# A transformer block pair on one core: low parts on GpSimd in the attention, filling products' splits later, a new opening, spread value products, sums between k-tiles

## The chip, the core and the metric

The kernel runs on one core of a Trainium2 chip. It has TensorE (PE in the profile, with PEld for its weight loads), VectorE (DVE), ScalarE (ACT), GpSimd (POOL) and the DMA queues, here those of SyncE (SP), ScalarE and GpSimd. The metric is the time of one execution on the device in microseconds.

## What is computed

Two transformer blocks on 512 tokens of width 1024. The first has a sparse attention, then a cross attention over 256 memory tokens, then a gated feed-forward network. With 512 tokens every selected block and every window covers all earlier tokens, so two of the attention's three branches are plain causal attentions over two sets of keys and values.

```python
h = rmsnorm(x, norm_mix_w)
q, kc, vc, ks, vs, kw, vw, gl = split(h @ nsa_w_in)          # 16 heads of 64, 4 groups of keys
gates = sigmoid(gl)                                          # three per head and token
k_cmp, v_cmp = gelu(blocks(kc) @ ck_w1) @ ck_w2, gelu(blocks(vc) @ cv_w1) @ cv_w2
o = gates[0] * softmax(q k_cmp) v_cmp + gates[1] * softmax(q ks) vs + gates[2] * softmax(q kw) vw
x = x + o @ nsa_w_out
x = x + memory_cross_attention(rmsnorm(x), rmsnorm(mem))     # ca_wq, ca_wkv, ca_wo
x = x + (silu(causal_conv3(h @ gate)) * (h @ val)) @ ffn_w_down
x = rmsnorm(x)
# second block
u, v, za, ab, ab_gate, zb, g_a, g_b = split(rmsnorm(x) @ w_in_2 + b_in)
merged = sigmoid(g_a) * (spatial_gating(u, v, za) @ w_pa) + sigmoid(g_b) * (conv31_branch(ab, ab_gate, zb) @ w_pb)
x = x + merged @ w_out
x = x + sigmoid(rmsnorm(x) @ w_ple_gate) * (p @ w_ple)
out = rmsnorm(x)
```

## The kernel before

Activations are kept transposed, 128 features on the partitions and 512 tokens in the free dimension, so a width of 1024 is a list of eight tiles, the k-tiles of a product. Every float32 operand `x` of a large product is split in two rounded parts: the high part by ScalarE, the low part (`x` less the high part) by VectorE. `mm` adds three products: high by high, high by low, low by high. `dense` (L196) makes one tile of 512 columns from eight k-tiles, 24 products.

`weight` (L163) loads a piece of 128 x 1024 into one of three raw buffers (`wr`), and ScalarE makes the high part (`wh`). The low part (`wl`) goes to GpSimd or VectorE by a running count of pieces: `eng = nc.gpsimd if self.pieces % 4 < self.share else nc.vector`. `share` is 0 at first, 4 in the second block from its start to the `w_pa` products, and 0 after them.

The RMS norms are put behind the products: the tile of squares is summed over features by one-column products with a tile of ones (`token_sum`, L219), GpSimd takes the power -0.5 (`rsqrt`), and TensorE transposes the result to all partitions (`bcast`), which ScalarE copies to SBUF as `rb`. `stat` does the sum and the power.

The opening (`nsa`, L287) loads x and the first two weight pieces in halves of 512 columns, on SyncE's and ScalarE's queues; for each of eight k-tiles it splits x and runs two products into `pk`, with the squares of x made two k-tiles later. Then come weight piece 10, the last squares, the product `px[0]`, `stat` into `rt`, the product with piece 11, and `rb`. `shifted` (L329) scales and shifts `pk` and `px`; `cmp_keys` (L394) and `cmp_values` (L409) compress them with four weight pieces each, and call one function of a list after each piece: keys, queries, `token_gates` and `gates_turned` (L358) in the one, `values` (L436) in the other, which accumulates over its four calls in four PSUM banks.

The attention has 32 units, two per head. `stage_a` (scores, minimum, exponential, and a multiplication by gate over denominator on GpSimd), `stage_b` (TensorE transposes, then splits) and `stage_c` (products with the values) are staggered: at step s of the loop, `stage_a` has been called up to unit s + 2, `stage_b` is called for s and `stage_c` for s - 1. Other work is called at set steps (`FILL`, L42) ahead of `stage_b`: the remaining queries and keys, `mem_init`, `mem_keys` (L715) and `mem_values` (L731). A filling job runs its product and directly behind it takes it out of PSUM and splits it.

The order of instructions on each engine is not that of the program alone. A planner at build time takes, for an engine that its costs say is free, the ready instruction that stands first in the program. The order is then fixed, and each engine runs its list in order. The program's place is a priority. All instructions are recorded by one helper, so the profile shows one line (L95) for nearly everything, and tile names tell the groups apart.

`residual` (L748) adds a product to x, splits the result and adds up its squares on GpSimd; its followers (`cross` L767, `ffn_up` L857, `block2` L882) run a first `dense` and then `stat`, in `block2` by `norms` (L888) for two sets of squares.

Of the kernel before, what the change touches and what calls it, by code (L numbers as in the profile page):

```python
# [17 lines left out]
P = 128  # L18
# [102 lines left out]
class Body:  # L121
# [74 lines left out]
    def dense(self, src, rhs, n=S, raw=None):  # L196
# [22 lines left out]
    def token_sum(self, acc, n):  # L219
# [7 lines left out]
        return ps  # L227

# [24 lines left out]
    def setup(self):  # L253
# [9 lines left out]
        nc.vector.memset(self.ones, 1.0)  # L263
        self.neghalf = c.tile([P, 8], F32, name="neghalf")
# [22 lines left out]
    def nsa(self):  # L287
# [17 lines left out]
        acc = []  # L305

        def square(k):
            sq = self.a()
            nc.scalar.activation(sq, x[k], AF.Square)
            if k < 2:  # L310
                acc.append(sq)
            else:
                (nc.vector if k % 2 else nc.gpsimd).tensor_tensor(acc[k % 2], acc[k % 2], sq, op=ALU.add)

        pk = [self.ps(), self.ps()]
        for k in range(KD):
            xs.append(self.split(x[k], self.vec("norm_mix", k)))
            if k % 4 == 0:
                w = [self.split(t[:, k * P:k * P + S]) for t in w0]
            s = slice(k % 4 * P, k % 4 * P + P)  # L320
            for j in range(2):
                self.mm(pk[j], (w[j][0][:, s], w[j][1][:, s]), xs[k], k == 0, k == KD - 1)
            if k >= 2:
                square(k - 2)
# [139 lines left out]

        def keys(b, pair):
            p = self.dense([I["nsa_w_in"][12 + 2 * b + pair]], xs)
            f = self.a()
            nc.vector.tensor_tensor(f, p, rb, op=ALU.mult)
            for u in range(2):
                s = slice(u * 64, u * 64 + 64)  # L470
                h, l = self.a(dt=F32R), self.a(dt=F32R)
                so = slice(64 - u * 64, 128 - u * 64)
                nc.scalar.copy(h[s], f[s])
                nc.vector.tensor_sub(l[s], f[s], h[s].bitcast(F32))
                for t in (h, l):
                    nc.gpsimd.dma_start(t[so].bitcast(F32), t[s].bitcast(F32))
                del t
                K[b, 2 * pair + u] = (h, l)
# [3 lines left out]
        def queries(m):  # L482
            p = self.dense([I["nsa_w_in"][m]], xs)
            f = F[m] = self.a()
            nc.vector.scalar_tensor_tensor(f, p, -0.125, rb, op0=ALU.mult, op1=ALU.mult)
            for u in range(2):
                q = self.a(dt=F32R)
                s = slice(u * 64, u * 64 + 64)
                so = slice(64 - u * 64, 128 - u * 64)
                nc.scalar.copy(q[s], f[s])  # L490
                nc.vector.tensor_sub(q[so], f[s], q[s].bitcast(F32))
                Q[2 * m + u] = q
# [124 lines left out]
        w = self.weight(I["nsa_w_in"][10], raw)  # L617
        del raw
        square(KD - 2)
        square(KD - 1)  # L620
        nc.vector.tensor_tensor(acc[0], acc[0], acc.pop(), op=ALU.add)
        px = [self.ps()]
        for k in range(KD):
            s = slice(k * P, (k + 1) * P)
# [687 lines left out]
```

## Time and profile before

| what | us |
|---|---|
| median of 3 runs | 1444.14 (1443.67 to 1444.43) |
| the profiled execution | 1447.17 |
| its span, first to last instruction | 1445.4 |
| TensorE busy | 1413.7 (98%) |
| VectorE busy | 924.0 (64%) |
| ScalarE busy | 644.9 (45%) |
| GpSimd busy | 421.1 (29%) |
| mean granted TensorE clock | 0.994 |

The span is shorter than the execution's time, which also has what lies around the first and last instruction. A product counts as busy until its modelled end, about 390 ns for 512 columns, though the next may start 227 ns after it; so a busy TensorE isn't one at its peak, and the number of products in a stretch tells more.

### The profile page before, as it was taken

The numbers are of one execution on the slowest core, as the hardware profiler recorded it, in microseconds if no ns is written. First come the engines' busy times: TensorE is split into PE (matmuls) and PEld (weight loads), VectorE is DVE, ScalarE is ACT, GpSimd is POOL, SyncE is SP. The second block draws the span as 40 slices with busy tenths as digits, with TensorE's granted clock in tenths as the row PEclk, the third lists the DMA queues.
The fourth block names the chain that finished last, engine by engine and source line by source line (L and its number), as shares of the span: only waits on it lengthen the run. The fifth ranks groups of instructions, "written<-read, shape, count | busy, mean of one in ns | idle before, by whom it ended". The sixth has DMA issues, their size and how long they took to land.

```text
span 1445.4 us, 18570 instructions
## 1 busy us (share of the span) xinstructions
PE 1413.7 (98%) x7010; PEld 1189.7 (82%) x7010; DVE 924.0 (64%) x1551; ACT 644.9 (45%) x1113; POOL 421.1 (29%) x367
## 2 busy tenths in 40 slices
PE   8899989999999999999999999999999999999997
PEld 6787878988888888888888888888887888888897
DVE  5958999996455455655543227995978574444564
ACT  5467768784344332332333234223244554432452
POOL 2222556551210221111111124544455440011223
PEclk9999999999999999999999999999999999999999
DMA  6531121214312323233233332332322222332331
GB/s 209 160 117 59 34 70 59 74 36 158 99 59 88 102 88 102 89 102 99 90 95 98 94 123 87 117 102 74 101 76 86 88 88 88 104 100 92 98 102 59
DMA packets 42681, 136.14 MB, mean 94 GB/s; under 512 B 5600, under 2 KB 8032, under 8 KB 42592
## 3 DMA queue, kind: packets, MB, share of 16 engines
q1 hardware_dynamic: 39856, 129.98, 28.8%
q0 software_dynamic: 1152, 3.15, 0.8%
q10 hardware_dynamic: 1584, 1.84, 0.4%
q8 instruction: 55, 0.90, 0.2%
q14 instruction: 34, 0.28, 0.1%
HBM read 129.70 MB, written 2.10 MB: 91 GB/s over the span
## 4 chain that ended last, share of the span: by engine, by line
PE 90%; DVE 6%; ACT 1%; issue 1%; POOL 1%; DMA 0%; SPq 0%; POOLq 0%; ACTq 0%; DVEq 0%
PE ps L95 90%; DVE a L95 4%; DVE wl L95 1%; ACT a L95 1%; POOL a L95 0%; DMA wr<-in_nsa_w_in_dram 0%; DVE ps L95 0%; ACT wh L95 0%; DVE s L95 0%; POOL wl L95 0%; SPq L95 0%; POOLq L1307 0%; POOL s L95 0%; DVE wh L95 0%; ACTq L95 0%
## 5 line engine op out<-in xcount | busy, mean ns | idle before, releaser
L95 PE MATMUL ps<-a,wh 128*128 128x512 f32 (+1 forms) x3120 | 954.8, 387 | 0.0
L95 PEld LDWEIGHTS ps<-a,wh 128*128 128x128 f32 x3120 | 581.4, 188 | 114.3 <-issue 0.5
L95 PE MATMUL ps<-a,wl 128*128 128x512 f32 (+1 forms) x1552 | 599.8, 386 | 1.4 <-POOL wl L95 1.4
L95 ACT CAST wh<-wr 128x1024 fp32r<-128x1024 f32 (+1 forms) x224 | 233.4, 1044 | 510.0 <-PE ps L95 314.9
L95 DVE TENSOR_TENSOR a<-ps,a 128x512 f32<-128x512 f32 (+6 forms) x292 | 173.8, 610 | 264.2 <-PE ps L95 209.8
L95 PEld LDWEIGHTS ps<-a,wl 128*128 128x128 f32 x1552 | 292.0, 188 | 59.5 <-POOL wl L95 1.8
L95 POOL TENSOR_TENSOR a<-a,a 128x512 f32<-128x512 f32 (+1 forms) x102 | 130.6, 1284 | 576.6 <-ACT a L95 461.4
L95 DVE TENSOR_TENSOR wl<-wr,wh 128x1024 fp32r<-128x1024 f32 x168 | 216.9, 1293 | 123.2 <-ACT wh L95 122.0
L95 PE MATMUL ps<-a,a 128*128 128x256 f32 (+4 forms) x1204 | 212.9, 323 | 7.9 <-ACT a L95 7.4
L95 PEld LDWEIGHTS ps<-a,a 128*128 128x128 f32 x1204 | 171.0, 192 | 26.0 <-ACT a L95 13.5
L95 POOL TENSOR_TENSOR wl<-wr,wh 128x1024 fp32r<-128x1024 f32 x56 | 134.8, 2409 | 167.1 <-ACT wh L95 167.1
L95 DVE SCALAR_TENSOR_TENSOR ps<-a,vecs,ps 128x501 f32<-128x501 f32 (+25 forms) x240 | 167.6, 736 | 3.2
L95 POOL TENSOR_TENSOR a<-a,s 128x512 f32<-128x512 f32 (+3 forms) x140 | 115.6, 853 | 174.2 <-DVE s L95 87.1
L95 DVE TENSOR_TENSOR a<-a,a 128x512 fp32r<-128x512 f32 (+3 forms) x168 | 116.4, 699 | 35.9 <-ACT a L95 25.0
L95 ACT CAST a<-a 128x512 fp32r<-128x512 f32 (+1 forms) x116 | 71.6, 621 | 82.6 <-DVE a L95 68.3
L95 ACT ACTIVATE a<-a 128x512 f32<-128x512 f32 (+1 forms) x114 | 61.9, 550 | 92.9 <-DVE a L95 92.6
L95 PE MATMUL ps<-wh,a 128*128 128x512 f32 (+1 forms) x320 | 94.9, 376 | 1.2 <-ACT a L95 1.2
L95 ACT ACTIVATE a<-ps,s 128x256 f32<-128x256 f32 (+4 forms) x148 | 77.5, 528 | 28.1 <-DVE s L95 25.3
L95 DVE SCALAR_TENSOR_TENSOR a<-a,vecs,a 128x511 f32<-128x511 f32 (+3 forms) x92 | 75.5, 824 | 4.3 <-ACT a L95 3.5
L95 ACT CAST a<-ps 128x384 fp32r<-128x384 f32 (+2 forms) x132 | 62.9, 488 | 33.3 <-PE ps L95 28.3
L95 PEld LDWEIGHTS ps<-wh,a 128*128 128x128 f32 x320 | 59.8, 194 | 12.0 <-ACT a L95 1.6
L95 PE MATMUL ps<-ident,a 128*128 128x128 f32 x372 | 56.8, 276 | 9.3 <-DVE a L95 8.6
(81 smaller groups left out, 677.2 us busy)
## 6 DMA issues: line engine op xcount, KB each, us to landing
wr<-in_w_in_dram SPq DMA_DIRECT2D x56, 512.0 KB, 3.6
wr<-in_ffn_gate_dram SPq DMA_DIRECT2D x22, 512.0 KB, 3.6
wr<-in_ffn_val_dram SPq DMA_DIRECT2D x22, 512.0 KB, 3.6
wr<-in_ffn_d_dram SPq DMA_DIRECT2D x16, 512.0 KB, 3.5
wr<-in_nsa_w_in_dram SPq DMA_DIRECT2D x14, 512.0 KB, 3.7
wr<-in_ca_wk_dram SPq DMA_DIRECT2D x8, 512.0 KB, 3.5
wr<-in_ca_wv_dram SPq DMA_DIRECT2D x8, 512.0 KB, 3.6
wr<-in_nsa_w_out_dram SPq DMA_DIRECT2D x8, 512.0 KB, 3.5
```

What stands on the lines that cost most here:

```text
L95: return lambda *a, **k: f(*[_raw(x) for x in a], **{n: _raw(x) for n, x in k.items()})
```

## The change

Constants: `FILL` loses its first entry and some steps move up; `SHARE` gets two more values, 1 for `cmp_keys` and `cmp_values` and 4 for the attention loop; after the loop the share is 0 again. Setup runs nine products of `ones` into a PSUM tile that nothing reads. In the opening the first two weight pieces come in columns 0 to 256, 256 to 512 and 512 to 1024, and the squares move behind weight piece 10. The transposes for `rb` stand behind the fifth k-tile of the second product.

```diff
-FILL = (0, 2, 8, 10, 4, 6, 12, 14, 14, 15, 17, 20, 23, 26, 30)
+FILL = (1, 8, 10, 3, 5, 12, 14, 14, 15, 17, 20, 23, 26, 30)
-SHARE = (4, 0)
+SHARE = (4, 0, 1, 4)
...
+        idle = self.ps((P, P))
+        for _ in range(9):
+            nc.tensor.matmul(idle, self.ones, self.ones, start=True, stop=True)
...
-        for c, ks in ((slice(0, S), (2, 4)), (slice(S, 2 * S), (5, 6, 7))):
+        chunks = {0: (0, 256), 2: (256, 512), 4: (512, 1024)}
+        for k, ks in ((0, (2,)), (2, (4,)), (4, (5, 6, 7))):
+            c = slice(*chunks[k])
             for i in range(2):
                 nc.sync.dma_start(w0[i][:, c], I["nsa_w_in"][8 + i][:, c])
-            for k in ks:
-                nc.sync.dma_start(x[k], I["x"][k])
+            for j in ks:
+                nc.sync.dma_start(x[j], I["x"][j])
...
+        px, acc = [], []
+        for j in range(2):
+            w = self.weight(I["nsa_w_in"][10 + j], raw)
+            raw = None
+            if j == 0:
+                for k in range(KD):
+                    sq = self.a()
+                    nc.scalar.activation(sq, x[k], AF.Square)
+                    if k < 2:
+                        acc.append(sq)
+                    else:
+                        (nc.vector if k % 2 else nc.gpsimd).tensor_tensor(acc[k % 2], acc[k % 2], sq, op=ALU.add)
...
+            px.append(self.ps())
+            for k in range(KD):
+                s = slice(k * P, (k + 1) * P)
+                self.mm(px[j], (w[0][:, s], w[1][:, s]), xs[k], k == 0, k == KD - 1)
+                if j == 1 and k == 4:
+                    rb = self.to_sbuf(self.bcast(rt, NT))
+            if j == 0:
+                self.stat(acc, out=rt)
```

`keys`, `queries`, `mem_keys` and `mem_values` run their products and return a function `rest`, which takes the result out of PSUM and splits it. In the loop `rest` is called behind `stage_b` and `stage_c`. `values(0)` moves into `cmp_keys`, the others one call forward, `gates_turned` into `cmp_values`, and `queries(2)` out of the loop. In `mem_keys` the sum of squares moves ahead of the products.

```diff
+            rests = [f(*args) for f, args in fill.get(s, [])]
             stage_b(s)
             if s:
                 stage_c(s - 1)
+            for rest in rests:
+                if rest:
+                    rest()
...
-        cmp_keys(ck, [lambda: keys(1, 0), lambda: queries(1), token_gates, gates_turned])
+        self.share = SHARE[2]
+        cmp_keys(ck, [lambda: keys(1, 0)(), token_gates, lambda: queries(1)(), lambda: values(0)])
...
         def mixed(q):
-            values(q)
+            if q == 0:
+                gates_turned()
+            if q < 3:
+                values(q + 1)
+            else:
+                queries(2)()
```

In `cross`, `ffn_up` and `block2` the one-column sums stand between the k-tiles of the first product instead of behind it. The first `w_pa` piece in the second block gets share 0.

```diff
+    def sums_within(self, accs, first):
+        ps = []
+        def one(q, i):
+            if i == 0:
+                ps.append(self.ps((P, NT)))
+            t = accs[q][0]
+            self.nc.tensor.matmul(ps[q][:, i:i + 1], t[:, i * P:(i + 1) * P], self.ones[:, 0:1], start=(i == 0),
+                                  stop=(i == NT - 1))
+            if i == NT - 1:
+                accs[q].clear()
+        side = [(first + i, [lambda q=q, i=i: one(q, i) for q in range(len(accs))]) for i in range(NT)]
+        return side, lambda: ps.pop(0)
...
                 self.mm(ps, (w[0][:, s], w[1][:, s]), rhs[k], k == 0, k == last)
+                for f in side.pop(k, ()):
+                    f()
...
-            p4 = self.dense(w_in(4, m), xs)
+            side = ()
             if m == 0:
-                r = norms()
+                side, sums = self.sums_within([acc, acc2], 4)
+            p4 = self.dense(w_in(4, m), xs, side=side)
...
+            self.share = SHARE[0] if m else 0
             p = self.dense([I["w_pa_2"][m]], ya)
+            self.share = SHARE[0]
```

## Rows read from the trace of the kernel before

**Rows 1.** The page: engines' busy time, share of the span, instructions.

```profile
PE 1413.7 (98%) x7010; PEld 1189.7 (82%) x7010; DVE 924.0 (64%) x1551; ACT 644.9 (45%) x1113; POOL 421.1 (29%) x367
```

**Rows 2.** Windows: stretch, us; busy (xcount) of PE, PEld, DVE, ACT, POOL; PEclk; DMA; GB/s.

```profile
0.00:22.00 22.00, 14.80 (x49) 11.40 (x50) 14.59 (x24) 15.68 (x25) 8.36 (x24) 1.00 0.75 250
...
35.00:70.00 35.00, 31.23 (x159) 26.18 (x158) 34.32 (x66) 16.41 (x24) 9.60 (x18) 0.99 0.56 158
...
115.00:306.00 191.00, 181.55 (x1153) 157.17 (x1152) 174.98 (x457) 144.33 (x379) 99.45 (x127) 1.00 0.19 58
306.00:870.00 564.00, 563.51 (x2593) 468.24 (x2594) 287.04 (x391) 209.35 (x314) 98.37 (x74) 1.00 0.31 97
```

**Rows 3.** Windows of a few us: the granted clock and the products.

```profile
9.00:14.00 5.00, 5.00 (x12) 3.90 (x13) 4.74 (x11) 5.00 (x10) 0.19 (x2) 1.00 1.00 373
16.00:21.00 5.00, 5.00 (x23) 4.14 (x23) 5.00 (x7) 5.00 (x8) 3.14 (x4) 1.00 0.55 194
70.00:75.00 5.00, 5.00 (x22) 4.85 (x23) 2.40 (x6) 3.85 (x7) 1.04 (x1) 0.50 0.43 129
...
875.00:878.00 3.00, 3.00 (x8) 2.33 (x8) 1.81 (x3) 0.00 (x0) 2.47 (x2) 0.50 0.52 124
```

**Rows 4.** Windows, the first 12 us: what DMA moved.

```profile
0.00:12.00 12.00, 4.80 (x10) 3.23 (x11) 5.07 (x13) 6.54 (x11) 2.73 (x18) 1.00 0.80 282
```

**Rows 5.** Timeline of the opening: start, us, engine, operation, count, idle before.

```profile
0.83 0.17 DVE L95 MEMSET ones<- 128x128 f32 x1 [0.83 <-PEq L1301]
...
8.18 0.62 ACT L95 CAST a<-wr 128x512 fp32r<-128x512 f32 x1 [2.69 <-DMA wr<-in_nsa_w_in_dram]
...
8.85 13.27 PE L95 MATMUL ps<-a,a 128*128 128x512 f32 x45 [1.66 <-ACT a L95]
...
28.62 1.96 POOL L95 TENSOR_TENSOR rt<-s,neghalf 128x4 f32<-128x4 f32 x1 [5.91 <-DVE s L95]
...
33.79 0.60 PE L95 MATMUL ps<-ident,rt 128*128 128x128 f32 x4
...
35.98 6.94 DVE L95 TENSOR_TENSOR a<-ps,a 64x512 f32<-64x512 f32 x12
```

**Rows 6.** Timeline of TensorE at 70 us.

```profile
69.76 1.94 PE L95 MATMUL ps<-fold,a 128*128 128x48 f32 x8 [2.55 <-ACT a L95]
```

**Rows 7.** Waits from 115 to 306: us, times, longest.

```profile
PE ps L95 <- DVE a L95: 7.5, 8, 2.3
```

**Rows 8.** VectorE's groups from 115 to 306: busy us, mean ns, idle before.

```profile
L95 DVE TENSOR_TENSOR a<-ps,a 128x384 fp32r<-128x384 f32 x52 | 28.0, 552 | 2.7 <-ACT a L95 2.5
L95 DVE TENSOR_TENSOR wl<-wr,wh 128x1024 fp32r<-128x1024 f32 x17 | 24.0, 1415 | 1.2 <-ACT wh L95 1.2
...
L95 DVE TENSOR_TENSOR a<-a,a 64x512 fp32r<-64x512 f32 x16 | 14.4, 899 | 0.4
```

**Rows 9.** VectorE's groups from 35 to 115.

```profile
L95 DVE TENSOR_TENSOR a<-a,a 64x512 fp32r<-64x512 f32 (+1 forms) x16 | 10.9, 688 | 0.3
```

**Rows 10.** GpSimd's groups from 880 to 1108.

```profile
L95 POOL TENSOR_TENSOR wl<-wr,wh 128x1024 fp32r<-128x1024 f32 x38 | 91.7, 2416 | 115.4 <-ACT wh L95 115.4
```

**Rows 11.** Timeline at 210 us: GpSimd, VectorE, TensorE.

```profile
207.27 5.19 POOL L95 TENSOR_TENSOR a<-a,s 128x128 f32<-128x128 f32 x5 [1.15 <-DVE s L95]
...
208.33 2.00 DVE L95 TENSOR_TENSOR wl<-wr,wh 128x1024 fp32r<-128x1024 f32 x1 [0.16 <-ACT wh L95]
...
210.36 2.65 DVE L95 TENSOR_TENSOR a<-a,a 64x512 fp32r<-64x512 f32 x2
...
213.78 0.55 PE L95 MATMUL ps<-ident,a 128*128 128x128 f32 x3 [2.29 <-DVE a L95]
```

**Rows 12.** Timeline at 870 us: GpSimd's additions, the one-column products.

```profile
869.86 2.98 POOL L95 TENSOR_TENSOR a<-a,a 128x512 f32<-128x512 f32 x2
...
871.85 2.10 PE L95 MATMUL ps<-ones,a 128*128 128x1 f32 x16
```

**Rows 13.** Timeline at 1111 us: TensorE's product with the low part.

```profile
1111.02 0.50 PE L95 MATMUL ps<-a,wl 128*128 128x512 f32 x1 [1.39 <-POOL wl L95]
```

More of the change, by code (lines that the diff above doesn't have):

```diff
@@ L317, in nsa @@
             xs.append(self.split(x[k], self.vec("norm_mix", k)))
-            if k % 4 == 0:
-                w = [self.split(t[:, k * P:k * P + S]) for t in w0]
-            s = slice(k % 4 * P, k % 4 * P + P)
+            if k in chunks:
+                c0, c1 = chunks[k]
+                w = [self.split(t[:, c0:c1]) for t in w0]
+            s = slice(k * P - c0, k * P - c0 + P)
             for j in range(2):
                 self.mm(pk[j], (w[j][0][:, s], w[j][1][:, s]), xs[k], k == 0, k == KD - 1)
-            if k >= 2:
-                square(k - 2)
         del w, w0
@@ L465, in keys @@
         def keys(b, pair):
[L466 to L478, printed above, removed]
+            p = [self.dense([I["nsa_w_in"][12 + 2 * b + pair]], xs)]
@@ new lines, in rest @@
+            def rest():
+                f = self.a()
+                nc.vector.tensor_tensor(f, p.pop(), rb, op=ALU.mult)
+                for u in range(2):
+                    s = slice(u * 64, u * 64 + 64)
+                    h, l = self.a(dt=F32R), self.a(dt=F32R)
+                    so = slice(64 - u * 64, 128 - u * 64)
+                    nc.scalar.copy(h[s], f[s])
+                    nc.vector.tensor_sub(l[s], f[s], h[s].bitcast(F32))
+                    for t in (h, l):
+                        nc.gpsimd.dma_start(t[so].bitcast(F32), t[s].bitcast(F32))
+                    del t
+                    K[b, 2 * pair + u] = (h, l)
@@ L480, in nsa @@
+            return rest
         Q, F = {}, {}
         def queries(m):
[L483 to L492, printed above, removed]
+            p = [self.dense([I["nsa_w_in"][m]], xs)]
@@ new lines, in rest @@
+            def rest():
+                f = F[m] = self.a()
+                nc.vector.scalar_tensor_tensor(f, p.pop(), -0.125, rb, op0=ALU.mult, op1=ALU.mult)
+                for u in range(2):
+                    q = self.a(dt=F32R)
+                    s = slice(u * 64, u * 64 + 64)
+                    so = slice(64 - u * 64, 128 - u * 64)
+                    nc.scalar.copy(q[s], f[s])
+                    nc.vector.tensor_sub(q[so], f[s], q[s].bitcast(F32))
+                    Q[2 * m + u] = q
@@ L494, in nsa @@
+            return rest
         outs = []
@@ L614, in dense_c @@
                 vcmp[g] = None
[L617 to L624, printed above, removed]
-            self.mm(px[0], (w[0][:, s], w[1][:, s]), xs[k], k == 0, k == KD - 1)
+        px, acc = [], []
[10 more added lines that the diff above has]
+                        (nc.vector if k % 2 else nc.gpsimd).tensor_tensor(acc[k % 2], acc[k % 2], sq, op=ALU.add)
+                    del sq
+                nc.vector.tensor_tensor(acc[0], acc[0], acc.pop(), op=ALU.add)
+                x.clear()
+            px.append(self.ps())
[6 more added lines that the diff above has]
+                self.stat(acc, out=rt)
         del w
-        x.clear()
-        self.stat(acc, out=rt)
-        px.append(self.dense([I["nsa_w_in"][11]], xs))
-        rb = self.to_sbuf(self.bcast(rt, NT))
         ck = shifted(pk)
-        keys(0, 0)
+        keys(0, 0)()
         cv = shifted(px)
-        queries(0)
+        queries(0)()
         units = [(h, b) for h in range(16) for b in range(2)]
@@ L679, in at @@
             fill.setdefault(s, []).append((f, a))
-        jobs = [(queries, 2), (queries, 3), (keys, 0, 1), (keys, 1, 1)] + [(queries, j) for j in range(4, 8)]
+        jobs = [(queries, 3), (keys, 0, 1), (keys, 1, 1)] + [(queries, j) for j in range(4, 8)]
         jobs += [(xs.clear,), (self.mem_init,)] + [(self.mem_keys, j) for j in range(4)] + [(self.mem_values, 0)]
@@ L685, in nsa @@
         self.banks = BANKS
+        self.share = SHARE[3]
         for s in range(n):
@@ L688, in nsa @@
                 stage_a()
-            for f, args in fill.get(s, []):
-                f(*args)
+            rests = [f(*args) for f, args in fill.get(s, [])]
             stage_b(s)
@@ L696, in nsa @@
         self.banks = {}
+        self.share = 0
         return outs
@@ L741, in mem_values, with rest @@
                             k == 0, k == KD - 1)
-        for i in range(2):
-            self.mv[i, hf] = self.split(pp[i], self.mrt[:, i:i + 1])
+        def rest():
+            for i in range(2):
+                self.mv[i, hf] = self.split(pp.pop(0), self.mrt[:, i:i + 1])
         if hf == 1:
             del self.ms, self.mrb
+        return rest
     def residual(self, src, rhs, x, gain, scale=None):
```

53 lines of the change are left out of this document (30 added, 23 removed).

## The prediction

> **What bounds the kernel now.** I read the engine totals first [rows 1]: TensorE is busy 1413.7 us of 1445.4, so nearly all the time is its products, and the change adds none but nine that run before the data arrive. What can be won is time in which TensorE waits or runs at half its rate, so the next view is the table by stretch [rows 2]. TensorE lacks 7.2 us in the first 22 us, 3.8 us from 35 to 70, 9.4 us from 115 to 306, and almost nothing in the 564 us behind that. The third view is the granted clock beside the number of products [rows 3]: 12 products of 512 columns in 9 to 14 us against 23 in 16 to 21, or 427 against 227 ns each by the spacing of their starts, the rates of 1.2 and 2.4 GHz. The clock record begins at 14.8 us, so the "1.00" of the first row is a default and the counts decide. Two more stretches show 0.50: around 70 to 75 and 875 to 878.
>
> Then, for each stretch, what TensorE waits for. In the opening: the second half of the first weights, which ScalarE splits from 8.18 on [rows 5]. At 67 to 70: ScalarE, 2.55 us [rows 6], while VectorE is busy 34.3 of 35 us [rows 2]. From 115 to 306: VectorE, 7.5 us in eight waits [rows 7], while VectorE is busy 175 of 191 us [rows 2]. So in the attention VectorE is a second bound just behind TensorE; GpSimd (99.5 of 191 us) and ScalarE (144 of 191) have room.
>
> The profiled execution took 1447.17 us: its span 1445.4 and 1.8 around it. The median of the runs is 1444.14, 3.0 lower. I work out a difference in the profiled execution and take it from 1444.14.
>
> **Part 1, the opening (gain 4.5 us).** Before, TensorE makes three products at 5.5, waits until 8.85, and runs the other 45 until 22.1 [rows 5]. Those between 8.85 and 14.6, some 13, ran at 427 ns, which cost 13 x 0.2 = 2.6 us. The change does two things. The weights' first pieces have 256 columns, so 0.26 MB instead of 0.52 stand ahead of the first six products; I expect them by some 5 to 6 us. And nine float32 products of `ones`, which is set at 1.0 us [rows 5], occupy TensorE ahead of the data, so the clock can rise earlier than at 14.6. What then limits is the data: x and the first weights are 3.15 MB, and 282 GB/s over the first 12 us [rows 4] bring that by 11.2 us; x[7] then needs its split and six products, some 3 us: 14.2 at the earliest. TensorE's own 48 products of 0.227 us need 10.9 us from 5 us on: 15.9. So the best is 15.9 against 21.9 (the last product's start), a gain of 6. The worst: the clock rises at 14.6 as before; from 5.5 us on 21 products fit ahead of it and 27 x 0.227 = 6.1 us follow, 20.7, a gain of 1.2. I take 4.5, nearer the first, because TensorE will still pause for data between 5 and 10 us and may be granted the clock late. The six squares that leave the opening come back while px[0] runs (24 products, 5.4 us), with GpSimd's additions behind them; a short wait before the sums is inside the bounds. The chunks add two DMA issues on SP ahead of x[5] to x[7], which TensorE doesn't need before some 12 us; I cost them at nothing, and at a microsecond if they hold x back.
>
> **Part 2, from `rb` to the values (gain 3.5 us).** `rb` was transposed only after the whole second product (33.79), though GpSimd had `rt` at 30.6, and VectorE's chain (`shifted`, then the key compression) began at 35.98 [rows 5]. After, the transposes stand behind five of eight k-tiles, 3 x 0.68 = 2.0 us earlier, beside part 1. The `gates_turned` products, for which TensorE waited 2.55 us [rows 6], stand several product groups behind their input, and values(0) comes forward as filling. The stretch at 0.50 right behind that wait [rows 3] held six 512-column products, 1.2 us. To win: 3.8 + 1.2 = 5.0 us. VectorE's own work shrinks by 3 low parts here (of the pieces 5 to 19 those divisible by 4), at most 1.4 us each [rows 8]; on GpSimd, nearly idle here, they hide. I take 3.5; bounds 0 and 5.
>
> **Part 3, the attention loop (gain 6 us).** All 19 weight pieces (5 queries, 2 keys, 8 memory keys, 4 memory values) give their low parts to GpSimd. VectorE now spends 24.0 us on 17 of them between 115 and 306 [rows 8]; without them it is busy 151 of 191. GpSimd's price is 2.42 us each [rows 10]: 46 us on top of 99.5, so 145 of 191; it still fits. But not all of the 24 us come back. VectorE's subtraction of two SBUF tiles takes 899 ns in this stretch [rows 8] and 688 from 35 to 115, where GpSimd computes little [rows 9]; its subtraction from PSUM takes 552 for 384 columns [rows 8]. In one place GpSimd does five multiplications in 5.19 us, and meanwhile a VectorE low part takes 2.00 us and two half-tile subtractions 2.65, and TensorE's transposes wait 2.29 us for that [rows 11]. Some 60 of VectorE's remaining instructions here read two SBUF tiles (20 subtractions, 8 of the memory split, 30 small ones). At 0.2 us (899 - 688) to 0.65 us (2.65/2 - 0.69) each that is 12 to 39 us, less the 12 they lose already. VectorE's net relief is therefore between 24 and -3 us; I take 12, about half.
>
> The Trainium skill, page "SBUF — State Buffer", section "Who interferes with whom", speaks against this part: a VectorE instruction with two SBUF inputs and a GpSimd instruction that reads SBUF share a port pair, and whoever comes second is blocked for the other's whole instruction. The trace agrees so far [rows 11]. By that rule alone a meeting would cost VectorE up to 2.4 us; what that could do to the time is the first rival.
>
> The other half of this part orders work: the splits of a filling product now follow stage_b and stage_c, so the chain that feeds the transposes goes ahead of them. In [rows 11] the transposes stand behind exactly such a low part and two query splits, 4.65 us. TensorE's 9.4 idle us here [rows 2], and short waits that the modelled ends hide, are the most there is to win. I take 6; bounds 12 and -23 (first rival).
>
> **Part 4, sums between k-tiles (gain 1.5 us).** At the second block's start 16 one-column products in a row take 1.9 us [rows 12], and the clock then shows 0.50: 8 products at 427 ns, 1.6 us [rows 3]. Spread behind k-tiles 4 to 7 there is no such row of narrow products. But the sums are then asked for from 869.8 us on (three k-tiles of 0.68 us ahead of the 16), and GpSimd's two additions end at 872.84 [rows 12]: if they hold TensorE's queue, all products behind them wait 3 us. The order of the engines' instructions follows readiness by a planner's costs, so I expect them later among the tiles. Bounds +1.7 and -3. In the two other places the count of products is the same and the clock record shows no dip: 0, or -0.8 each if the sum holds TensorE for one k-tile.
>
> **Part 5, first w_pa piece on VectorE (gain 1.2 us).** TensorE waited 1.39 us for GpSimd's low part [rows 13]; VectorE needs about half of GpSimd's time. Bounds 1.4 and 0, if VectorE's taps are ahead of it.
>
> Sum: 4.5 + 3.5 + 6 + 1.5 + 1.2 = 16.7; 1444.14 - 16.7 = 1427.4.
>
> **Rivals.** First, GpSimd becomes the bound of the loop (slower). Its multiplications feed the transposes and queue in order behind low parts of 2.42 us; each of these also blocks VectorE. For: 145 of 191 us busy, [rows 11]. Against: stage_a runs two units of some 6 us ahead, and 38 low parts from 880 to 1108 [rows 10] cost TensorE almost nothing. If a low part costs TensorE half its length, 1.2 us, that is 23 us; with the other parts' 10.7 us won the time is 1444.1 + 12.3 = 1456.4. It decides from 10.7 / 19 = 0.56 us per low part on. Chance 0.09.
>
> Second, the opening and the loop keep less than half: the clock rises late (part 1: 1.2 us) and the port eats VectorE's relief (part 3: 2 us). 1.2 + 2 + 3.5 + 1.5 + 1.2 = 9.4: 1434.7. For: pauses for data between 5 and 10 us; 0.65 us per meeting. Against: TensorE, if slow, has no pauses. Chance 0.20.
>
> Third, the sums between the tiles hold TensorE (part 4: -3 - 1.6 instead of +1.5): 1427.4 + 6.1 = 1433.5. Against: an order planned by readiness. Chance 0.05.
>
> Fourth, the change doesn't do what it says: the planner weaves the splits as before, and VectorE's chain from 36 to 70 takes back the opening. Parts 4 and 5 remain, 2.7 us: 1441.4. Against: that chain starts earlier too. Chance 0.06.
>
> **How the numbers follow.** The forecast has 0.60, its own range 1420 to 1434 (parts 1 to 3 each off by a few us). Leaving out the first rival (0.09), the fourth (0.06) and some 0.05 below (part 1 at 6 and part 3 at 12 or so), the range is 1417 to 1440. A measurement of this kernel tells 0.2%, 2.9 us, from no change: faster takes the forecast and the second and third rivals, 0.85; the same is the fourth, 0.06; slower the first, 0.09.
>
> **What would show it.** Part 1: 512-column products at 227 ns before 14.6 us, the 48th before 18.5. Part 2: `shifted` on VectorE before 30 us, no TensorE wait near 65, no 0.50 there. Part 3: no VectorE low parts in the loop, TensorE idle there under 5 us, two-SBUF subtractions above 1000 ns. Part 4: no 0.50 near 860. Part 5: no wait on `wl` near 1095. The prediction is wrong if TensorE's waits in the loop are on GpSimd, or if its products are still at 427 ns at 14 us.

## The result, and the profile after

The change is slower: 1462.24 us (median of 4 runs, 1458.85 to 1464.03) against 1443.91, a ratio of 1.0125 [1.0102, 1.0147]. The prediction was 1427.4 with a range of 1417 to 1440, and 0.85 on faster; it was wrong in sign, by a change of 1.2%.

The profiled execution took 1460.5 us, 13.3 more than that of before (1447.17); the medians differ by 18.3, because the profile of before lies 3 us above its median and that of after 1.7 below; so 5 of the 18 us are in no trace. Engine totals of the kernel after, to be set against [rows 1]:

```profile
PE 1421.5 (97%) x7028; PEld 1195.6 (82%) x7028; DVE 913.1 (63%) x1532; ACT 646.1 (44%) x1115; POOL 460.8 (32%) x388
```

Work moved as planned: GpSimd has 39.7 us more, VectorE 10.9 less. TensorE's products are the same but for the 18 records of the nine products of `ones` (a float32 product leaves two records), so the place of the loss can be read by pairing records: pair them from the last one back and subtract the start of each in the trace of before from its start in that of after. The numbers count from 0 in the trace of before. In the loop some filling products have changed places, so from 864 to 1700 a pair has the same count behind it, but is not always the same product.

```
product      48    528    672    864   1220   1260   1700   1800   2700   4400   7000
before, us  22.0  118.9  146.1  180.2  243.6  249.4  313.0  332.0  518.7  903.2 1434.7
after, us   -2.9   -6.0   -4.8   -3.7   -0.9   +3.4   +3.0   +5.2   +7.0  +12.9  +13.2
```

So the opening and the stretch behind it win 6.0 us. The attention loop loses 11.2: 5.1 bit by bit to 244 us, 4.3 at one place near 245, 2.2 at its end near 332. Behind it 7.7 go in three steps (0.9, 0.9 and 5.9), at the three places where sums now stand between k-tiles. The windows of after, with the columns of [rows 2, 3]:

```profile
0.00:22.00 22.00, 20.26 (x80) 16.70 (x81) 16.30 (x28) 16.20 (x27) 7.88 (x24) 1.00 0.80 272
9.00:14.00 5.00, 5.00 (x21) 4.06 (x20) 5.00 (x13) 4.88 (x9) 0.41 (x2) 1.00 1.04 366
35.00:70.00 35.00, 32.45 (x165) 27.23 (x164) 33.10 (x62) 20.00 (x28) 10.82 (x14) 1.00 0.60 157
70.00:75.00 5.00, 5.00 (x36) 4.49 (x35) 3.61 (x6) 2.70 (x4) 2.16 (x4) 1.00 0.58 183
115.00:306.00 191.00, 175.83 (x1106) 153.42 (x1104) 157.50 (x428) 138.30 (x365) 122.28 (x140) 0.98 0.17 50
306.00:870.00 564.00, 560.58 (x2582) 465.07 (x2581) 285.79 (x390) 208.38 (x315) 99.73 (x75) 1.00 0.32 97
880.00:890.00 10.00, 10.00 (x32) 8.36 (x33) 2.62 (x4) 1.04 (x1) 3.37 (x3) 0.52 0.10 30
```

From 9 to 14 us there are 21 products where there were 12, and the stretch at 0.50 behind 70 us is gone. From 115 to 306 VectorE is busy 17.5 us less, and TensorE makes 1106 products instead of 1153; the granted clock was 0.50 there twice, for 3.4 us from 180.6 and from 245.4 us. TensorE waits there for these (us in total, times, longest), to be set against [rows 7]:

```profile
PE ps L96 <- DVE a L96: 11.1, 10, 2.4
PE ps L96 <- POOL s L96: 2.8, 1, 2.8
PE ps L96 <- ACT a L96: 0.8, 2, 0.4
```

An engine with less to do is waited for more. Three groups of VectorE in that stretch say why ([rows 8] has the first and the last of them), with GpSimd's low parts below:

```profile
L96 DVE TENSOR_TENSOR a<-ps,a 128x384 fp32r<-128x384 f32 x52 | 28.0, 549 | 4.5 <-ACT a L96 4.3
L96 DVE TENSOR_TENSOR a<-a,a 64x512 fp32r<-64x512 f32 x14 | 17.5, 1251 | 0.4
L96 DVE TENSOR_TENSOR s<-s,gates 128x4 f32<-128x4 f32 x27 | 9.9, 365 | 0.6
...
L96 POOL TENSOR_TENSOR wl<-wr,wh 128x1024 fp32r<-128x1024 f32 x13 | 31.9, 2461 | 1.7 <-ACT wh L96 1.6
```

Subtractions with one input in PSUM take what they took (549 against 552 ns). Those with both inputs in SBUF went from 899 to 1251.

These means hide few and long meetings: of the 14 subtractions two stand beside a low part for all of its length and take 2.76 and 2.93 us, where one alone takes 0.69; the other slow ones, 0.99 to 1.43, stand beside multiplications (one of them partly beside a low part), as those of before do (up to 1.52). Of the 27 products with the gates five meet a low part and take 0.32 to 2.20 us, where one alone takes 0.17.

One meeting, from the timeline of after (start, us, engine):

```profile
208.40 3.65 DVE L96 TENSOR_TENSOR a<-a,a 64x512 fp32r<-64x512 f32 x2
208.40 2.38 POOL L96 TENSOR_TENSOR wl<-wr,wh 128x1024 fp32r<-128x1024 f32 x1
...
212.08 1.27 DVE L96 TENSOR_TENSOR a<-ps,a 128x384 fp32r<-128x384 f32 x2
...
212.69 0.55 PE L96 MATMUL ps<-ident,a 128*128 128x128 f32 x3 [2.35 <-DVE a L96]
```

Two query splits and GpSimd's low part start together. The first split's record is 2.93 us long, GpSimd's 2.38 plus 0.55; the second takes 0.69. The splits that the transposes need (128x384, from PSUM) stand behind them in VectorE's order, and TensorE waits 2.35 us. That is no loss against before, where VectorE's own low part stood at this place and the wait was 2.29 us [rows 11]; it is relief that was not won. At 175 us a low part and two query splits meet in the same way: TensorE waits 2.03 us where before it waited 1.24, and the first of the two stretches at 0.50 follows.

The Trainium skill, page "SBUF — State Buffer", section "Who interferes with whom" and, on the lock, "SBUF: two separate sides", states that a VectorE instruction with two SBUF inputs contends with a GpSimd instruction that reads SBUF and that the loser is held for the whole of the other; one with at most one SBUF input, outside VectorE's two-port modes, doesn't contend. These records agree on both counts (2.38 + 0.55 us; 549 ns).

### The profile page after: what moved, and what is told of

It is laid out like the page before. It is cut to its first block, busy times and chain, and to the rows that moved or that the text cites. A ratio compares the mean times of both kernels' runs of the same rounds, so it can differ in the third digit from the quotient of the medians.

```text
span 1458.5 us, 18590 instructions
## 1 busy us (share of the span) xinstructions
PE 1421.5 (97%) x7028; PEld 1195.6 (82%) x7028; DVE 913.1 (63%) x1532; ACT 646.1 (44%) x1115; POOL 460.8 (32%) x388
## 5 line engine op out<-in xcount | busy, mean ns | idle before, releaser
L96 DVE TENSOR_TENSOR a<-ps,a 128x512 f32<-128x512 f32 (+7 forms) x292 | 173.5, 609 | 275.4 <-PE ps L96 214.0
L96 DVE TENSOR_TENSOR wl<-wr,wh 128x1024 fp32r<-128x1024 f32 (+1 forms) x147 | 189.2, 1288 | 120.7 <-ACT wh L96 119.7
L96 POOL TENSOR_TENSOR wl<-wr,wh 128x1024 fp32r<-128x1024 f32 x77 | 188.3, 2449 | 194.8 <-ACT wh L96 194.7
L96 DVE TENSOR_TENSOR a<-a,a 128x512 fp32r<-128x512 f32 (+3 forms) x168 | 124.5, 747 | 35.7 <-ACT a L96 25.0
L96 POOL TENSOR_TENSOR a<-a,s 128x512 f32<-128x512 f32 (+3 forms) x140 | 104.9, 779 | 131.4 <-DVE s L96 111.5
```

Source lines behind the costliest of these rows:

```text
L96: return lambda *a, **k: f(*[_raw(x) for x in a], **{n: _raw(x) for n, x in k.items()})
```

## The experiments

The parts were separated first. In the expectations, S is the theory that the sums between the tiles cost, P that of the port that VectorE and GpSimd share, M that the earlier sum of the memory's squares costs, Q that GpSimd's queue as such does, W that the sums wait for GpSimd's additions, and C that the lone narrow products bring the clock down.

**e1_sums_behind.** The sums of `cross`, `ffn_up` and `block2` stand behind the first product again (here `cross`; the other two alike).

```diff
-    side, sums = self.sums_within([acc], 4)
 p = [self.dense([I["ca_wq"][2 * h]], xs, side=side)]
-    r = self.rsqrt(sums(), NT, 1.0 / D, 1e-6)
+    r = self.stat(acc)
```

> The changed kernel with one part undone: in cross, ffn_up and block2 the one-column sums stand behind the first product again. Theory S (the sums, issued in the program's place, hold TensorE's queue until GpSimd's last addition, and in block2 the thinned products bring a longer stretch at 1.2 GHz): of the 13.1 us that the profiled span of the changed kernel lies above that of before, 7.6 us arise at these three places (0.9, 0.9 and 5.8), so the time falls by 7 to 9 us, to about 1454. Rival L (all of the loss is made in the attention loop and later differences only shift it): no change, 1462 +- 2.

1451.54, ratio 1.0059 [1.0042, 1.0077]: 10.7 us of the loss, more than the 7 to 9 that were expected and than the 7.7 of the trace. S holds, and L (all of the loss is made in the loop) falls.

**e9_sums_second.** The sums stay between k-tiles, but of the second product, four k-tiles later than in after.

```diff
-    side, sums = self.sums_within([acc], 4)
-p = [self.dense([I["ca_wq"][2 * h]], xs, side=side)]
+p = [self.dense([I["ca_wq"][2 * h]], xs)]
+    side, sums = self.sums_within([acc], 0)
+p.append(self.dense([I["ca_wq"][2 * h + 1]], xs, side=side))
```

> The changed kernel with the one-column sums of cross, ffn_up and block2 between the k-tiles 0 to 3 of the second product instead of 4 to 7 of the first, when GpSimd's additions are long done. If the wait for GpSimd is what cost (theory W), it is as fast as or up to 2 us faster than e1_sums_behind (1451.5), with no waits at the sums and a granted clock of 1.00 around block2's start. If thin products between wide ones bring 1.2 GHz by themselves (theory C), block2's start still shows 0.50 for several us and the time is 2 us above e1.

1451.06, 1.0048 [1.0033, 1.0064], the same as e1. The timelines show what differs. First after, where [rows 12] has the 16 records of the sums in a row:

```profile
876.89 2.92 POOL L96 TENSOR_TENSOR a<-a,a 128x512 f32<-128x512 f32 x2
878.64 0.38 PE L96 MATMUL ps<-ones,a 128*128 128x1 f32 x2 [1.67 <-POOL a L96]
879.87 0.38 PE L96 MATMUL ps<-ones,a 128*128 128x1 f32 x2 [0.84 <-POOL a L96]
```

Then e9_sums_second:

```profile
874.01 2.99 POOL L96 TENSOR_TENSOR a<-a,a 128x512 f32<-128x512 f32 x2
...
876.66 0.77 PE L96 MATMUL ps<-ones,a 128*128 128x1 f32 x4
```

```profile
870.00:885.00 15.00, 14.75 (x77) 12.23 (x76) 4.02 (x8) 5.33 (x7) 10.02 (x7) 1.00 0.39 123
```

In after TensorE's queue stands for 2.5 us behind additions that aren't done, and then the clock is at 1.2 GHz for 10.2 us (0.52 in the window of 880 to 890, against 3.4 us of it in before). In e9 as many narrow products stand between wide ones, TensorE doesn't stand, and the clock stays at 2.4 GHz. So W holds and C falls: the lone narrow products don't bring the clock down; here it fell behind the waits. (A row of them doesn't decide it either: e7_open_only below has the same 16 records in a row as before, at 870.5 us, and no 0.50 there.)

**e2_loop_vector.** The loop's low parts go back to VectorE.

```diff
-SHARE = (4, 0, 1, 4)
+SHARE = (4, 0, 1, 0)
```

> The changed kernel with the attention loop's share at 0: all low parts of the loop on VectorE again, the rest of the change kept. Theory P (port: GpSimd's 2.4 us low parts block VectorE's two-SBUF instructions, which stand ahead of the splits that feed the transposes): TensorE's waits on VectorE in the loop (2.0, 2.35 us and so on) go, the time falls by 4 to 10 us; two-SBUF subtractions of half tiles fall from 1251 to about 900 ns. Rival O (the loss in the loop comes from the new order: splits behind the attention's steps, queries(2) and values moved out): the time stays within 2 us or grows, since VectorE gets 19 low parts back (1.2 us each).

1450.65, 1.0044 [1.0027, 1.0061]: 11.6 us of the loss, a little more than the 4 to 10 expected; the half-tile subtractions are back at 838 ns, and the jump at 245 us is gone too.

**e8_port.** GpSimd is as occupied as in after, but reads nothing: each low part of the loop is replaced by five zero fills (the low parts of the loop's weights are left out).

```diff
+if self.hold:
+    for q in (0, 1, 0, 1, 0):
+        nc.gpsimd.memset(lo[:, q * S:(q + 1) * S].bitcast(F32), 0.0)
+    return hi, lo
```

> The changed kernel with GpSimd's low parts in the attention loop replaced by five fills of 128x512 with zeros each (some 2.6 us of GpSimd time, but nothing is read from SBUF; these low parts are zero, so that part of the products is left out in value, not in time). Theory P (port: reading low parts block VectorE's two-SBUF instructions): VectorE's half-tile subtractions fall from 1251 to 900 ns or less, TensorE's waits on VectorE in the loop go, the time falls by 6 to 11 us, near e2 (1450.7). Rival Q (GpSimd's occupied queue makes its multiplications late): the time stays within 3 us of 1462.

1443.42, 0.9993 [0.9983, 1.0002]: 18.8 us less than after, with the slow sums still in; 6 to 11 were expected. Its groups from 115 to 306:

```profile
L96 DVE TENSOR_TENSOR a<-a,a 64x512 fp32r<-64x512 f32 x14 | 11.6, 829 | 0.4
...
L96 DVE TENSOR_TENSOR s<-s,gates 128x4 f32<-128x4 f32 x28 | 5.0, 179 | 0.6
...
L96 POOL MEMSET wl<- 128x512 f32 x75 | 35.9, 524 | 0.0
```

GpSimd spends 35.9 us on fills against 31.9 on low parts, and VectorE's groups are back at 829 and 179 ns. The Trainium skill's page "SBUF — State Buffer", section "Who interferes with whom", says that such a VectorE instruction doesn't contend with a GpSimd instruction that only writes; this run agrees. P holds for the larger part of it. Q falls for the multiplications: in after, too, they start 0.24 us on average behind the VectorE product that they wait for (0.22 in before). But the fills wait for no weights, so the run also takes away lateness of the low parts themselves: the waits at 245 and 332 us are 0.50 and 0.28 us here. Of the 16.9 us that its trace lies ahead of after's at product 2700, 5.5 arise at these two places, where it was GpSimd that was late; at most the other 11.4 are the port's.

**e14_bound.** e8_port with e9's sums: what the change could give without both losses.

> The kernel after with the sums in the second product (as in e9_sums_second) and with the loop's low parts on GpSimd replaced by five zero fills each (as in e8_port; the weights' low parts in the loop are zero, so that part of the result is left out). If the two losses are separate, their reliefs add: after 1462.2, less 18.8 (e8_port) and less 9 to 11 (e1, e9) gives 1432 to 1435, and this is what the change would have given had GpSimd's instructions not slowed VectorE's and the sums not waited. If both runs took away the same loss, it stays at 1441 to 1444.

1435.08, 0.9928 [0.9915, 0.994], at the edge of what was expected. The reliefs add nearly in full: 27.2 us together, where e8's 18.8 and e9's 11.2 make 30.0. It leaves out work that has to be done somewhere, so it is a bound and not a version.

**e4_memsum, e3_at_once, e5_comb, e6_comb_at_once.** e4 puts the memory's sum back between its products; e3 calls every `rest` at once behind its product.

```diff
-rests = [f(*args) for f, args in fill.get(s, [])]
+rests = []
+for f, args in fill.get(s, []):
+    rest = f(*args)
+    if rest:
+        rest()
+    del rest
```

> The changed kernel with the memory tokens' sum of squares back between the two products of mem_keys(0). Theory M (the sum ahead of the products sends the power and the transposes forward, so that the transposes wait in TensorE's queue for GpSimd, which is busy with two low parts and four multiplications: 2.8 us, and 3.4 us at 1.2 GHz behind it): the jump of 4.2 us at 245 us goes, the time falls by 3 to 5 us. Rival P (GpSimd's low parts alone make it late, wherever the sum stands): the jump stays, within 1 us.

> The changed kernel with the filling products' splits called directly behind their products in the loop, as before; GpSimd keeps the loop's low parts. Theory P (port): the order hardly matters, as the planner puts the query splits ahead of the transposes' splits in either case: within 3 us. Rival O (new order costs): the time falls by 5 us or more. Third: the new order helps, the time grows by 3 us or more.

1460.54, 1.0114 [1.0099, 1.0129], and 1460.62, 1.012 [1.0105, 1.0135]: neither matters beyond the spread of the runs. M falls; the jump at 245 us stays in e4 (4.4 us), and the power of the memory's norm stands on GpSimd behind two low parts and four multiplications in both (in e4 from 236.4 us on). In after:

```profile
237.72 4.75 POOL L96 TENSOR_TENSOR wl<-wr,wh 128x1024 fp32r<-128x1024 f32 x2
...
242.43 2.77 POOL L96 TENSOR_TENSOR a<-a,s 128x128 f32<-128x128 f32 x4
...
245.14 0.72 POOL L96 TENSOR_TENSOR s<-s,neghalf 128x2 f32<-128x2 f32 x1
...
245.92 0.69 PE L96 MATMUL ps<-ident,s 128*128 128x128 f32 x2 [2.81 <-POOL s L96]
```

e5 is e1, e2 and e4 together, e6 is e5 with e3.

> The changed kernel with three parts undone: the sums behind the first products (as in e1), the loop's low parts on VectorE (as in e2) and the memory sum between its products (as in e4); opening, spread values, splits that follow and w_pa stay. Theory: the two losses add (10.7 and 11.6 us at the medians against 1462.2), so about 1440, 4 us under the kernel before. Rival: they overlap (a stall in the loop only moves what the sums would wait for), 1444 to 1450.

> e5_comb with the filling products' splits directly behind their products, so that of the change opening, spread values, queries(2) ahead of the loop and w_pa are left. If the splits that follow cost where VectorE makes the low parts (e2 still lost 3.1 us in the loop against before), it is 2 to 4 us faster than e5_comb; if they help, slower; as with GpSimd's low parts (e3), no difference beyond 2 us.

1442.81, 0.9991 [0.998, 1.0002], and 1443.99, 0.9996 [0.9987, 1.0006]. e5 lies between its theory and its rival: 19.4 us come back where the two losses make 22.3. The order of the splits makes no difference here either. With both losses undone what is left of the change, the opening among it, is worth nothing that can be measured.

**e7_open_only.** Before, with the new opening alone (chunks of 256 columns, the nine products, the squares behind, `rb` between k-tiles).

> The kernel before with the opening of the change alone (first weights in chunks of 256 columns, nine products of ones, squares behind the opening, rb between k-tiles). Theory: the 2.9 us that the trace of after shows at the 48th product, and about as much from rb to the keys, are kept to the end: 1438 to 1441. Rival: VectorE's chain from 36 to 70 us takes it back, 1442.5 to 1444.5.

1445.35, 1.0002 [0.9993, 1.0011]; outside the theory's range and 0.9 us above the rival's. Its trace starts product 48 4.3 us and product 192 5.9 us earlier than before, product 304 (78 us) 4.4, product 864 1.6 and product 1220 1.3. From 61 to 68 us TensorE waits 2.7 us for VectorE's low parts, where before has no such wait. In the loop TensorE now waits for VectorE 10.7 us where [rows 7] has 7.5:

```profile
PE ps L95 <- DVE a L95: 10.7, 9, 2.3
```

So the opening is real, and most of it is given back where VectorE's chain, not TensorE, sets the pace: 1.6 us from 66 to 78 us, 3.1 from 104 us on, in the attention. At its end this trace is still 2.9 us ahead (the 3.4 us at half rate at 875 us don't occur in it), but the medians show nothing left.

**e19_before_again.** The kernel before, profiled again.

> The kernel before, unchanged, profiled a second time. Its first profile lies some 3 us above its median. If that 3 us lies in one stage, it tells which offsets against the first profile are the execution's and not the edit's; if the second profile agrees within 1 us at each stage, the offsets of the opening-only kernel (4.3 at the 48th product, 1.3 at the end of the loop) are its own.

1447.28 us, and each product of the table above starts within 0.1 us of the first profile. So before's first profile was no odd one, and the offsets don't come from it. The timed runs left no trace, but their mean granted clock is on record: of 107 runs of before, the 27 at 0.994 took 1445.9 us on average and the 22 at 0.997 took 1442.7. Both profiles are at 0.994, so most of the 3 us above the median goes with the clock of the execution; in which stretch stays open. Nor is one profile of an edit exact: of the 18 that have the new opening, two (after and e2) start product 48 2.7 to 2.9 us earlier than before, the others 4.2 to 5.2.

**e12_in_psum.** With e9's sums and GpSimd's low parts kept, all queries and keys, those ahead of the loop too, and the memory keys are scaled in place in PSUM and split from there, so that VectorE's subtractions have one SBUF input (here the queries).

```diff
-f = F[m] = self.a()
-nc.vector.scalar_tensor_tensor(f, p.pop(), -0.125, rb, ...)
+f = p.pop()
+nc.vector.scalar_tensor_tensor(f, f, -0.125, rb, ...)
 ...
+F[m] = self.to_sbuf(f)
```

> The kernel after with the sums in the second product, GpSimd keeps the low parts of the loop, but keys, queries and memory keys are multiplied in place in PSUM, ScalarE and VectorE split them from there (ScalarE copies the queries for the compressed scores), so that no subtraction of VectorE in the loop reads two SBUF tiles but the memory's own split. Port theory: what delays the loop are the 64x512 subtractions (1251 ns against 688 without GpSimd beside them) in front of the splits of the transposes; from PSUM they take 680 ns whatever GpSimd does, the waits of 2.0 to 2.4 us of TensorE on VectorE in the loop go, and the time falls from e9's 1451 to 1437 to 1445 (the small gates products still meet GpSimd). Rival: the low parts cost by their place in GpSimd's queue, or by VectorE's work as such; then it stays at 1449 to 1452.

1445.15, 0.9997 [0.9987, 1.0006]: 5.9 us less than e9 by the medians, 7.4 by the ratios (1.0048), just outside the expected range and far from the rival's. It is less than half of the 16 us between e9 and e14_bound. From 115 to 306:

```profile
L96 DVE TENSOR_TENSOR a<-ps,a 64x512 fp32r<-64x512 f32 x14 | 9.6, 688 | 0.4
...
L96 DVE TENSOR_TENSOR s<-s,gates 128x4 f32<-128x4 f32 x27 | 9.4, 349 | 0.5
...
L96 POOL TENSOR_TENSOR wl<-wr,wh 128x1024 fp32r<-128x1024 f32 x15 | 35.8, 2392 | 2.0 <-ACT wh L96 1.9
```

The subtraction takes 688 ns on average and 695 at most, beside the same low parts; the gates products, still with two SBUF inputs, stay at 349.

**e13_in_psum_mem, e16_quarters, e17_in_psum_values** are e12 with one more edit each: the first memory key's low part on VectorE; GpSimd's low parts in four instructions of 256 columns; the memory values' low parts on VectorE (`if s == FILL[-1]: self.share = 0`).

> e12_in_psum, with the low part of the first memory key piece back on VectorE, so that the power of the memory's norm doesn't stand behind it on GpSimd. Theory: the wait of 2.8 us and the stretch at the lower clock behind it near 245 us go, 2 to 4 us below e12_in_psum. Rival: the power waits behind the four multiplications anyway; same as e12_in_psum within 1 us.

> e12_in_psum with each low part that GpSimd makes in the loop issued as four instructions of 256 columns. If an instruction of VectorE is held for the whole of the GpSimd instruction that it meets, shorter ones hold it less: the small gates products (365 ns against 177) and the memory's split get faster, and the time falls by 1 to 4 us below e12_in_psum (1445.2). If both just share the time, the sum of GpSimd's work is the same and each instruction adds its own start: same as e12_in_psum or up to 2 us more.

> e12_in_psum with the low parts of the four memory value pieces at the end of the loop back on VectorE. In e12_in_psum TensorE waits 2.2 us at 322.7 us for the last of them, which stood behind four multiplications on GpSimd, and runs 3.4 us at half rate after it; between products 1700 and 1800 it loses 3.8 us against the kernel before. Theory: this goes, 1441 to 1443. Rival: VectorE is as late with them, 1444.5 to 1446.

e13: 1448.29, 1.0019 [1.001, 1.0028], a miss; two other low parts stand ahead of the power on GpSimd then (from 233.3 us on), and TensorE's wait on it is 3.6 us. So its question isn't answered. e16: 1443.98, 0.9999 [0.999, 1.0008], the same as e12; the gates products stay at 350 ns on average and GpSimd needs 42.2 us for 15 pieces instead of 35.8, so shorter instructions win nothing. In one meeting a product of 128x4 elements is held through all four of them:

```profile
240.96 2.97 DVE L96 TENSOR_TENSOR s<-s,gates 128x4 f32<-128x4 f32 x1
...
241.11 2.79 POOL L96 TENSOR_TENSOR wl<-wr,wh 128x256 fp32r<-128x256 f32 x4
```

e17: 1442.38, 0.9983 [0.9974, 0.9992], as expected.

**e15_psum_vector, e18_loop_psum, e20_loop_psum_vector.** e15 is e12 with the loop's low parts on VectorE. e18 and e20 are e17 and e15 with the splits in PSUM for the loop's own pieces alone (`f = p[0] if self.banks else self.a()`).

> e12_in_psum with all low parts of the loop on VectorE (as before the change). It tells what reading the splits from PSUM is worth by itself. Port theory: without GpSimd's low parts a subtraction from SBUF costs VectorE as much as one from PSUM (688 against 680 ns), so this is e5_comb again, 1441 to 1444. Rival: the multiplications of GpSimd alone hold VectorE enough that PSUM splits win, 1436 to 1440.

> e17_in_psum_values with the splits in PSUM only for the pieces of the loop itself; the keys and queries ahead of it go through SBUF as in the kernel after. In e12, e16, e17 and e15 alike TensorE loses 4 to 7 us between products 528 and 672 (118.9 to 146.1 us), where the transposes wait three times about 1.4 us for VectorE, and e9 and e14_bound, which split through SBUF there, don't lose them. Theory: the query split just ahead of the loop, in PSUM, stands in the way of the transposes' splits; 1438 to 1441. Rival: the loss is handed on to the next place where VectorE is the bound; 1441.5 to 1443.5.

> e15_psum_vector (low parts of the loop on VectorE) with the splits in PSUM only for the pieces of the loop itself. Theory as for e18_loop_psum: the 7 us that e15 loses between products 528 and 672 stay away, at least in part; 1437 to 1441. Rival: VectorE is the bound of the loop with its low parts, so the loss comes later; 1441.5 to 1443.5. If it is not above e18_loop_psum, GpSimd's low parts in the loop are worth nothing even with splits that it can't hold up.

1442.35, 0.9986 [0.9977, 0.9995]; 1443.07, 0.999 [0.9982, 0.9999]; 1440.10, 0.9969 [0.9958, 0.998]. e15 and e20 came as expected. e18 missed its 1438 to 1441: it still loses 4.3 us from product 528 to 672, and so does e20 (4.5), so the query split ahead of the loop is not the whole cause of that. The record shows what the loss is made of: in every version with splits in PSUM TensorE waits two or three times in a row there (in e20 0.79, 1.93 and 1.06 us, at 118 to 124 us), and the clock is at 1.2 GHz for 6.8 us from 121 us on (10.2 in e13 and e15), as it isn't in e9 and e14. From e20:

```profile
121.00:128.00 7.00, 5.08 (x13) 3.95 (x14) 6.33 (x20) 4.30 (x16) 3.28 (x5) 0.53 0.01 4
```

Why the waits stand there stays open.

e20 is the fastest complete version: all the loop's low parts on VectorE, none on GpSimd. From 115 to 306 it has

```profile
sum 191.00, PE 182.43 PEld 158.35 DVE 168.69 ACT 146.29 POOL 97.53; mean PE 182.43 PEld 158.35 DVE 168.69 ACT 146.29 POOL 97.53
```

```profile
PE ps L96 <- DVE a L96: 5.5, 6, 1.9
```

and e18, with the low parts of the loop but for the last four pieces on GpSimd:

```profile
sum 191.00, PE 180.04 PEld 158.03 DVE 159.44 ACT 143.24 POOL 118.05; mean PE 180.04 PEld 158.03 DVE 159.44 ACT 143.24 POOL 118.05
```

```profile
PE ps L96 <- DVE a L96: 7.5, 8, 1.8
```

VectorE is 9.3 us busier in e20, and TensorE waits 2 us less for it.

## Why the prediction was wrong

**Part 3, the loop, is the step that failed.** The prediction booked the port as load of VectorE. It took 0.2 to 0.65 us for each of some 60 meetings off VectorE's 24 us of relief, was left with 12, and turned half of that into time. VectorE's load did fall by 17.5 us, more than the 12 that were taken (e8_port, which gets through more products in the same window, has it at 157.2 too). But load was not what TensorE waits for: it waits for the splits of its transposes, which have one SBUF input and don't slow down (549 ns), yet stand in VectorE's queue behind query and key splits that do.

And the meetings with low parts are fewer and longer than was priced: a full one costs a subtraction 2.1 to 2.2 us at that moment (at 175 and 208 us), not 0.2 to 0.65, and the idle time that the lighter load leaves later doesn't give it back. TensorE idles 15.2 of the 191 us, where under 5 were forecast. From product 528 to 1800 the trace loses 11.2 us where 6 were to be won. The bound of 12 to -23 held that, the value didn't. How the 11.2 divide between the port, the late low parts and the clock is shown only in part: 4.3 and 2.2 arise at 245 and 332 us, where a low part made GpSimd itself late; the 5.1 before that are longer waits on VectorE and 3.4 us at half rate, which cost 1.7.

The first rival came nearest (1456.4), with a loss twice that of the loop (-23 us) and mostly another mechanism: that GpSimd becomes the bound, though it names the blocking of VectorE beside that. The waits from 115 to 306 us are mostly on VectorE, 11.1 us of 14.7, and e8_port fills GpSimd as much at no cost. It holds at two places only: the power at 245 us, 2.8 us, and a low part at 332 us that TensorE waits 2.18 us for.

The order of splits, the other half of part 3, was to save up to 9.4 us. In e3_at_once and e6_comb_at_once it makes no difference.

**Part 4 failed too.** The sums were expected "later among the tiles" because the planner orders by readiness. They were issued at k-tiles 4 to 7, and the third rival, with a chance of 0.05, happened: 5.9 us at the second block (2.5 of waits and 10.2 us at half rate, less the 3.4 at half rate that before has), where 3 were the bound, and 0.9 in each of the two other places, where 0.8 was; 7.7 together, where 4.6 were its price. e1 and e9 give 10.7 and 11.2 back.

**Part 1** was right as far as its own stretch goes: 21 products from 9 to 14 us, and the 48th 2.9 us earlier in after and 4.3 in e7, against 4.5. In after it begins at 18.8, not before 18.5, as the products start 427 ns apart until 9.9 us; in e7 they start 230 apart from 6.8 us on. What failed is that it was added to the end: alone it wins nothing there (1.0002 [0.9993, 1.0011]). The fourth rival had VectorE's chain take it back at 36 to 70 us; some of that shows in e7 (1.6 us behind its waits at 61 to 71), but the larger part is taken back in the attention. **Part 2** came as foreseen: a further 3.1 us by product 528 against 3.5, no wait and no 0.50 near 70 us (but one wait of 2.05 us at 59, for a low part of VectorE); that, too, is lost in the loop. **Part 5** won nothing: the wait of [rows 13] became one for VectorE, the lower bound that was named.

```profile
1117.73 0.50 PE L96 MATMUL ps<-a,wl 128*128 128x512 f32 x1 [1.14 <-DVE wl L96]
```

The sum in the trace: -6.0 (parts 1 and 2) + 11.2 (part 3) + 7.7 (part 4) + 0.3 (part 5) = 13.2 us.

## What to carry to other kernels

Before work is moved from VectorE to GpSimd, look at what stands in VectorE's queue ahead of the instructions that TensorE waits for: if those have two inputs in SBUF, each meeting delays the chain by up to the length of GpSimd's instruction, and VectorE's falling load hides it in a table of busy time, as a mean hides it in a table of groups: look at the single records. Such splits are safe if they read PSUM (688 instead of 1251 ns), and here the low parts were better left on VectorE. A small product placed between large ones was free only where its input was done when TensorE got there; if not, everything behind it waits and the clock may fall with it, so place it late rather than early. And a gain ahead of a stretch that another engine paces has to be followed to the end before it is counted.

## What was not expected of the hardware

- Of 27 VectorE products of 128x4 elements with two SBUF inputs, 0.17 us alone, five that met a low part in after took 0.32 to 2.20 us, until GpSimd's instruction ended (mean of all 365 ns, beside fills 179). Cutting GpSimd's instruction from 2392 to 737 ns didn't lower the mean (350): one was held for four in a row, 2.97 us.
- After 2.5 us of waits in two pieces at 878 to 880 us the granted clock was at 1.2 GHz for 10.2 us, with wide and narrow products alternating; after a single wait of 2.81 us at 245 us it was for 3.4, after one of 2.03 at 179 us for 3.4 too, and after one of 2.35 at 212.7 us not at all.
- Two profiles of the same kernel agree within 0.1 us at every product compared, while its timed runs spread over 1441.5 to 1447.4, with the mean granted clock (1445.9 us on average at 0.994, 1442.7 at 0.997).
